# A two-layer hybrid decoder trunk on one core: forget logits two slots later, the first products of a normed operand in another order, six output chunks by halves

## The chip, the cores and the metric

The kernel runs on one core of one Trainium2 chip. The metric is the device time of one execution in microseconds (us). Each core has engines with instruction queues of their own: TensorE (PE in the profile, its weight loads are PEld), VectorE (DVE), ScalarE (ACT), GpSimd (POOL) and SyncE (SP), which here issues most of the DMAs.

## The reference

The input x has 512 positions of 1024 features in float32; there are two layers with their own weights.

```python
for l in range(DEPTH):
    mod = (c_act @ ada_w[l] + ada_b[l])[:, None, :]
    sh1, sc1, g1, sh2, sc2, g2 = jnp.split(mod, 6, axis=-1)
    h = rmsnorm(x, norm_mix_g[l]) * (1.0 + sc1) + sh1
    u = h @ w_in[l]
    fq, fk, fv, ff, pu, rq, rk, rv, rg, cu = jnp.split(u, bounds, axis=-1)
    y_fox = fox_attention(fq, fk, fv, ff, fox_fb[l])      # 4 heads of 64; log_sigmoid(ff) is summed over the positions
    y_pool = pool_mixer(pu, pool_w[l], pool_scale[l])
    y_ret = retention(rq, rk, rv, rg, positions, ret_gn_g[l])
    y_conv = conformer_conv(cu, conv_w[l], conv_b[l], conv_ln_g[l], conv_ln_b[l])   # depthwise, 31 taps
    mix = jnp.concatenate([y_fox, y_pool, y_ret, y_conv], axis=-1)
    x = x + g1 * (mix @ w_out[l])
    h = rmsnorm(x, norm_ffn_g[l]) * (1.0 + sc2) + sh2
    f = (jax.nn.silu(h @ ffn_w1[l]) * (h @ ffn_w3[l])) @ ffn_w2[l]
    x = x + g2 * f
return rmsnorm(x, final_g)
```

(The reshapes into heads are left out here.)

## The kernel before, in words

**Layout.** x is held transposed in `xT`, as eight chunks of 128 features by 512 positions. Each large product is made from three fp32r matmuls: every operand is split into a high part, rounded to fp32r, and a low part, the remainder. `mm3` issues high times high, high times low and low times high. For the normed operand the parts are `yh[k]` and `yl[k]`, k = 0 to 7; for a weight `wh` and `wl`; for an activation `ah` and `al`.

**Weights.** `plan` lists all weight tiles in order of use. `load_w` fetches one by DMA into `raw` (two buffers), casts it on ScalarE into `wh` (L179) and subtracts on VectorE into `wl` (L184); `wh` and `wl` have four buffers each. `take` hands out the next tile, `rel` gives a buffer back, which starts the load of a later tile.

**Order.** All of TensorE's instructions after the opening stand in program order (`keep_in_program_order`). On the other engines the framework's scheduler sets the order at build time. Work that is not a large product is written as generators: `fox_gen` (forgetting attention), `ret_gen` (retention), `conv_gen` (convolution), `ada_pe_gen` (the modulation vector of layer 0 on TensorE), and others. `slot()` stands between groups of products and lets each running generator advance by a rate: `r_...` in layer 0, `q_...` in layer 1. A rate of 1.3 means 1.3 steps a slot on average. A step runs from one `yield` to the next. `finish_bg` runs a generator to its end at once. `do_o`, the first half of the output projection, begins with `finish_bg([cg])`, which ends the convolution.

**Norm.** `Norm.chunk` squares and adds each finished chunk of `xT`, by halves of 256 positions. When the eighth chunk of a half is there, `pending` gets `sums` (token sums on TensorE, reciprocal root on VectorE and GpSimd) and then `finish` (the root is spread by TensorE; per chunk k: `mod_t` makes t on VectorE, `mod_hi` makes yh on ScalarE, `mod_lo` makes yl on VectorE). `flush(n)` takes n from each pending counter and runs what reaches zero; its calls stand between matmuls.

**Output projection, second half.** Of its eight chunks the first N1 are made together over all 512 columns, a few singly, and the last NH by halves of the columns, first all lower halves and then all upper halves, so that the lower half's norm can start while the upper halves are made. NH is 5 before.

**First products after a norm.** `group` makes four products (i = 0 to 3) that read the whole normed operand, lower half first, then upper half. It stands after norm 1 of layer 1 and after norm 2 of both layers. It is also used, by halves, for the last four chunks of the second feed-forward product.

**Forget logits.** `fox_gen` first runs `log_forget` on the logits ff (a chain of small VectorE and ScalarE instructions, L818 to L828), yields twice, and then sums the result over positions with twenty small matmuls (`sm<-cs,ff` and `sm<-ones,ff` in the trace).

Of the kernel before, what the change touches and what calls it, by code (L numbers as in the profile page):

```python
# [31 lines left out]
SEGS = (8, 7, 7)  # L32
PIECE = 1040
TW = 528
KN = {'GA': 3, 'GA1': 3, 'TR': 'V', 'NH': 5, 'NH1': 5, 'ST': ((0, 1), (1, 1), (2, 2), (4, 1), (5, 1), (6, 1), (7, 1)), 'MO': 'rk rq rv pu rg o o o o', 'MO1': 'rk rq rv pu rg o o o o', 'GK': 4, 'RD': 'sync', 'MM': 3, 'SM': 4, 'FB': 1, 'FB1': 1, 'OUTP': 0.0, 'FRONT': 1, 'FRONT1': 0, 'r_rot': 2, 'r_ada': 0.9, 'r_conv': 1.3, 'r_fox': 1, 'r_ret': 1, 'r_pool': 1, 'r_adaV': 0.4, 'q_conv': 1.3, 'q_fox': 1, 'q_ret': 1, 'q_pool': 1, 'q_adaV': 1, 'bP': 4, 'bPT': 2, 'bt': 3, 'brx': 2, 'bmx': 6, 'br8': 4, 'bpl': 3, 'brP': 4, 'bada': 3, 'bacs': 2, 'NR': 2, 'NW': 4, 'N1': 3, 'N11': 1, 'YLG': 9, 'SC': ('AVPPPGPA', 'GGPAVVPP', 'VVVVVVPP', 'VVVVVGVP', 'AAVPAVVP', 'VVVVVVVP', 'VVVVVVVP', 'AAVPAVVP'), 'SH': ('AVAPPPPP', 'VPPPPPAP', 'AAGAAAPP', 'AAAAAAPP', 'AAAAAAGP', 'AVVGAAVG', 'AAAAAAPP', 'AAAAAAPP'), 'MS': '', 'OF': {'lc': -1.907, 'lwq': -2.817, 'lw': -2.364, 'lh': -2.036, 'sc': -1.65, 'ds': 0.034, 'sh': -2.846, 'pc': -0.763, 'mc': -2.466, 'ph': -0.991, 'mh': 0.907, 't': 0.871, 'yh': -1.858, 'yl': 0.927, 'wh': -0.208, 'wl': -2.386, 'whq': -1.469, 'wlq': -0.219, 'mm': 0.333, 'mq': -0.566, 'dq': 0.84}, 'KB': (-4.084, -0.552, 1.672, 3.163, 4.202, 4.915, 6.134, 7.492), 'OA': (1, 0, 2, 3), 'OA1': (0, 1, 3, 2), 'OB': (1, 2, 0, 3), 'OB1': (1, 3, 0, 2), 'OUTP1': 3.0}
# [11 lines left out]
def trunk(ctx, tc, x, c, positions, ada_w, ada_b, norm_mix_g, norm_ffn_g, w_in, fox_fb,  # L47
# [240 lines left out]
    FULL = ((0, S),)  # L288
    HALF = ((0, H2), (H2, S))

    def group(n, th, tl, nk, cols, done):
        ws = [take() for _ in range(n)]
        banks = banks4()[:n]
        for (a, b) in cols:
            for i in range(n):
                h, lo = ws[i]
                for k in range(nk):
                    if k % 2:
                        flush()
                    mm3(banks[i][:, a:b], h[:, k], lo[:, k], th[k][:, a:b], tl[k][:, a:b],  # L300
                        k == 0, k == nk - 1)
                done(i, banks[i], a, b)
                if b == S:
                    rel()
                slot(2.0 * (b - a) / S)
# [74 lines left out]
    def ada_pe_gen(l, parts):  # L380

        js = [part * KD + jj for part in parts for jj in range(KD)]
        ld = [ada_load(l, js[0], 0, KD, 1), ada_load(l, js[1], 0, KD, 1)]
        acc = None
        for n in range(len(js) + 1):
            yield
            if acc is not None:
                pt = aux_cols(1)
                PE.matmul(pt, acc[:, 0:P], sel[:, 0:1], start=True, stop=True)
                ada_set(l, js[n - 1], 1, pt)  # L390
                gate1[0] += n == KD and l == 0
            if n == len(js):
                break
            r = ld.pop(0)
            pt = small()
            for half in range(2):
                for q in range(4):
                    k = 4 * half + q
                    PE.matmul(pt[32 * q:32 * q + 32, 0:P], cact[:, k:k + 1].to_broadcast([P, 32]), r[:, k],
                              start=half == 0, stop=half == 1)  # L400
            acc = tmp("pw")
            A.copy(acc, pt[:, 0:P])
            if n + 2 < len(js):
                ld.append(ada_load(l, js[n + 2], 0, KD, 1))
# [59 lines left out]
    def mod_t(l, i, k, u, v, rs):  # L464
        y = tmp("t", v - u)
        V.scalar_tensor_tensor(out=y, in0=xT[:, k, u:v], scalar=gs[l][i][:, k:k + 1], in1=rs,  # L466
                               op0=ALU.mult, op1=ALU.mult)
        return y
# [8 lines left out]
    def mod_lo(l, i, k, u, v, y):  # L477
        sh = shift(l, i, k)
        V.scalar_tensor_tensor(out=yl[k][:, u:v], in0=y, scalar=sh, in1=f(yh[k][:, u:v]), op0=ALU.add, op1=ALU.subtract)  # L479

    def modulate(l, i, k, u, v, rs):
        y = mod_t(l, i, k, u, v, rs)
        mod_hi(l, i, k, u, v, y)
        mod_lo(l, i, k, u, v, y)
# [635 lines left out]
    for l in range(DEPTH):  # L1120
# [166 lines left out]
        for si, nseg in enumerate(SEGS):  # L1287
# [102 lines left out]
```

## Time and profile before

| what | value |
|---|---|
| median of 3 runs | 1255.21 us (1253.73 to 1256.19) |
| the profiled execution: its own time | 1255.84 us |
| the profiled execution: its span | 1254.0 us |
| TensorE busy | 1204.4 us, 96% |
| VectorE busy | 735.8 us, 59% |
| ScalarE busy | 413.4 us, 33% |
| GpSimd busy | 71.8 us, 6% |
| mean granted clock of TensorE | 0.977 |

The span is the time from the first to the last instruction in the profile; the execution's own time is a little longer. Busy shares are means over stages with different limits. In a row of the timeline stand the start, the duration, the engine, the line, the operation, what it writes and reads, the shape and how many; in brackets, how long the engine sat idle before it and what ended that. The line of a TensorE row is that of the helper (L59), so such rows are told apart by the tiles that they name.

### The profile page before, as it was taken

What the parts mean: (1) busy time and instruction counts of PE and PEld (TensorE: products, weight loads), DVE (VectorE), ACT (ScalarE), POOL (GpSimd) and SP (SyncE); (2) the same over time, 40 slices, a digit from 0 to 9 for tenths busy, and PEclk for the clock granted to TensorE, in tenths of its full rate; (3) what the DMA queues carried; (4) which work ended last, traced back from release to release, by engine and by line L of the source; (5) the groups of instructions that cost most, each with busy time, mean ns of one, the idle gap of its engine ahead of it and who ended that gap; (6) DMA issues with size and microseconds to landing.
All of it is one profiled execution on the core that took longest, in us unless ns stands there. A gap on an engine that the chain in (4) does not pass through costs nothing.

```text
span 1254.0 us, 17311 instructions
## 1 busy us (share of the span) xinstructions
PE 1204.4 (96%) x6757; PEld 1000.4 (80%) x6757; DVE 735.8 (59%) x1314; ACT 413.4 (33%) x690; POOL 71.8 (6%) x146
## 2 busy tenths in 40 slices
PE   8997999989999999999989799998999999999997
PEld 8875776789888888888889777688988888888877
DVE  5869865577986373553467976747743333333333
ACT  5433344344222232132334334524432123213222
POOL 5401011001000000000000000100100000000000
PEclk7998999989999999999999989998999999999999
DMA  9785741226977363443333341222633323233321
GB/s 309 191 214 156 205 136 55 68 85 202 288 245 222 95 205 105 134 149 95 90 85 81 88 114 56 68 67 84 189 114 101 100 85 99 88 99 101 95 74 67
DMA packets 240873, 160.07 MB, mean 128 GB/s; under 512 B 7094, under 2 KB 221328, under 8 KB 240792
## 3 DMA queue, kind: packets, MB, share of 16 engines
q1 hardware_dynamic: 240616, 158.89, 43.1%
q8 instruction: 53, 0.87, 0.3%
q14 instruction: 28, 0.23, 0.1%
q10 hardware_dynamic: 176, 0.08, 0.0%
HBM read 154.74 MB, written 2.11 MB: 125 GB/s over the span
## 4 chain that ended last, share of the span: by engine, by line
PE 84%; DVE 8%; DMA 4%; ACT 2%; issue 1%; SPq 1%; POOL 0%; DVEq 0%; ACTq 0%; POOLq 0%
PE mm L59 74%; PE sm L59 8%; DVE hc L788 3%; DMA ad<-in_ada_w 1%; DMA raw<-in_w_in 1%; DVE wl L184 1%; PE aux L59 1%; PE sm L64 1%; ACT wh L179 1%; DMA rx<-rx 1%; DMA xn<-in_x 0%; DVE t L466 0%; DVE xT L1109 0%; DVE yl L479 0%; SPq L363 0%
## 5 line engine op out<-in xcount | busy, mean ns | idle before, releaser
L179 ACT CAST wh<-raw 128x1024 fp32r<-128x1024 f32 (+3 forms) x196 | 198.8, 1014 | 597.6 <-PE mm L59 423.5
L59 PE MATMUL mm<-yh,wh 128*128 128x512 f32 (+1 forms) x984 | 378.7, 388 | 7.9 <-ACT yh L475 7.9
L59 PE MATMUL mm<-yl,wh 128*128 128x512 f32 (+1 forms) x984 | 374.8, 381 | 4.3 <-DVE yl L479 4.3
L59 PE MATMUL mm<-yh,wl 128*128 128x512 f32 (+1 forms) x984 | 372.9, 379 | 0.0
L184 DVE TENSOR_TENSOR wl<-raw,wh 128x1024 fp32r<-128x1024 f32 (+3 forms) x196 | 231.8, 1183 | 159.2 <-ACT wh L179 148.8
L59 PEld LDWEIGHTS mm<-yh,wh 128*128 128x128 f32 x984 | 188.0, 192 | 46.6 <-ACT yh L475 8.7
L59 PEld LDWEIGHTS mm<-yl,wh 128*128 128x128 f32 x984 | 189.3, 192 | 39.7 <-DVE yl L479 5.5
L59 PEld LDWEIGHTS mm<-yh,wl 128*128 128x128 f32 x984 | 188.8, 192 | 36.4
L59 PE MATMUL mm<-ah,wh 128*128 128x512 f32 (+1 forms) x516 | 189.6, 368 | 0.0
L59 PE MATMUL mm<-al,wh 128*128 128x512 f32 (+1 forms) x516 | 188.3, 365 | 0.8 <-DVE al L521 0.8
L59 PE MATMUL mm<-ah,wl 128*128 128x512 f32 (+1 forms) x516 | 188.1, 365 | 0.0
L1109 DVE SCALAR_TENSOR_TENSOR xT<-mm,mod,xT 128x512 f32<-128x512 f32 (+1 forms) x86 | 58.0, 676 | 143.9 <-PE mm L59 143.8
L59 PEld LDWEIGHTS mm<-ah,wh 128*128 128x128 f32 x516 | 97.0, 188 | 17.7 <-issue 0.7
L59 PEld LDWEIGHTS mm<-al,wh 128*128 128x128 f32 x516 | 97.0, 188 | 17.7 <-DVE al L521 1.1
L59 PEld LDWEIGHTS mm<-ah,wl 128*128 128x128 f32 x516 | 97.0, 188 | 16.8
L1293 DVE TENSOR_TENSOR t<-t,mm 128x512 f32<-128x512 f32 x42 | 28.8, 687 | 109.1 <-PE mm L59 109.0
L788 DVE SCALAR_TENSOR_TENSOR hc<-hp,cwT,hc 128x512 f32<-128x512 f32 x120 | 83.2, 745 | 0.2
L339 DVE SCALAR_TENSOR_TENSOR acs<-ada,cact,acs 128x512 f32<-128x512 f32 x98 | 73.4, 749 | 6.0 <-DMA ada<-in_ada_w 3.4
L445 POOL TENSOR_TENSOR r<-r,mhalf 128x2 f32<-128x2 f32 (+3 forms) x16 | 20.1, 1255 | 625.2 <-DVE r L453 625.2
L475 ACT ACTIVATE yh<-t,mod 128x256 fp32r<-128x256 f32 (+1 forms) x56 | 27.8, 533 | 32.1 <-DVE t L466 29.8
L59 PE MATMUL mm<-wh,yh 128*128 128x256 f32 (+1 forms) x128 | 37.4, 292 | 0.0
L59 PE MATMUL mm<-wl,yh 128*128 128x256 f32 (+1 forms) x128 | 36.1, 282 | 0.0
(249 smaller groups left out, 1152.2 us busy)
## 6 DMA issues: line engine op xcount, KB each, us to landing
raw<-in_ffn_w SPq DMA_DIRECT2D x104, 512.0 KB, 3.9
ada<-in_ada_w SPq DMA_DIRECT2D x80, 512.0 KB, 4.6
raw<-in_w_in SPq DMA_DIRECT2D x32, 512.0 KB, 4.5
raw<-in_ffn_w SPq DMA_DIRECT2D x32, 448.0 KB, 3.7
ad<-in_ada_w SPq DMA_DIRECT2D x32, 256.0 KB, 5.8
raw<-in_w_out SPq DMA_DIRECT2D x32, 256.0 KB, 3.1
raw<-in_w_in SPq DMA_DIRECT2D x4, 520.0 KB, 7.1
xn<-in_x SPq DMA_DIRECT2D x4, 512.0 KB, 4.7
```

What stands on the lines that cost most here:

```text
L59: m = nc.tensor.matmul(*a, **kw)
L64: m = nc.tensor.transpose(*a, **kw)
L179: A.copy(h[:, 0:n], raw)
L184: V.tensor_tensor(out=lo[:, 0:n], in0=raw, in1=f(h[:, 0:n]), op=ALU.subtract)
L339: V.scalar_tensor_tensor(out=acc, in0=r, scalar=ck, in1=acc, op0=ALU.mult, op1=ALU.add)
L445: G.tensor_tensor(out=out_, in0=ms, in1=mhalf[:, 0:ms.shape[-1]], op=ALU.pow)
L475: A.activation(yh[k][:, u:v], y, AF.Identity, bias=shift(l, i, k), scale=1.0)
L788: V.scalar_tensor_tensor(out=hcs[j], in0=hps[j][:, t:t + S], scalar=cwT[:, l, j, t:t + 1], in1=hcs[j], op0=ALU.mult, op1=ALU.add)
L1109: V.scalar_tensor_tensor(out=xT[:, n, u:v], in0=b[:, u:v], scalar=mod[l][:, gcol + n:gcol + n + 1], in1=xT[:, n, u:v], op0=ALU.mult, op1=A ...
L1293: V.tensor_tensor(out=t_, in0=t_, in1=b3, op=ALU.mult)
```

## The change

It has these parts:

- `fox_gen` yields four times in place of twice between `log_forget` and the sums.
- `group` has a flag `first`, set at the three places after a norm. With it, the lower half goes k by k over all four products with the two terms that read yh, and then product by product over the terms that read yl. The upper half goes product by product, with all yh terms ahead of all yl terms.
- `finish` makes t and yh for all eight chunks and then yl for all eight; t lies in the `qk` buffers (four of 512 columns, two t each) in place of `t` (three buffers).
- The counters of `pending` and the arguments of `flush` go from 3, 4 and 1 to 18, 24 and 6 (4 inside the new loops).
- NH goes from 5 to 6, N1 of layer 0 from 3 to 2.
- `ada_pe_gen` collects eight columns in the `aux` bank and writes them to `mod` with one instruction.
- The rate of the convolution goes from 1.3 to 1.1 in layer 0 and from 1.3 to 1.2 in layer 1.

```diff
-KN = {... 'NH': 5, 'NH1': 5, ... 'r_conv': 1.3, ... 'q_conv': 1.3, ... 'N1': 3, ...}
+KN = {... 'NH': 6, 'NH1': 6, ... 'r_conv': 1.1, ... 'q_conv': 1.2, ... 'N1': 2, ...}
...
-    def group(n, th, tl, nk, cols, done):
+    def group(n, th, tl, nk, cols, done, first=False):
         ws = [take() for _ in range(n)]
         banks = banks4()[:n]
         for (a, b) in cols:
+            early_half = first and a == 0
+            if early_half:
+                for k in range(nk):
+                    for i in range(n):
+                        if i % 2 == 0:
+                            flush(4)
+                        h, lo = ws[i]
+                        PE.matmul(banks[i][:, a:b], h[:, k], th[k][:, a:b], start=k == 0, stop=False)
+                        PE.matmul(banks[i][:, a:b], lo[:, k], th[k][:, a:b], start=False, stop=False)
+                for i in range(n):
+                    h, lo = ws[i]
+                    for k in range(nk):
+                        if k % 4 == 0:
+                            flush(4)
+                        PE.matmul(banks[i][:, a:b], h[:, k], tl[k][:, a:b], start=False, stop=k == nk - 1)
             for i in range(n):
                 h, lo = ws[i]
-                for k in range(nk):
-                    if k % 2:
-                        flush()
-                    mm3(banks[i][:, a:b], h[:, k], lo[:, k], th[k][:, a:b], tl[k][:, a:b],
-                        k == 0, k == nk - 1)
+                if first and not early_half:
+                    for k in range(nk):
+                        PE.matmul(banks[i][:, a:b], h[:, k], th[k][:, a:b], start=k == 0, stop=False)
+                        PE.matmul(banks[i][:, a:b], lo[:, k], th[k][:, a:b], start=False, stop=False)
+                    for k in range(nk):
+                        PE.matmul(banks[i][:, a:b], h[:, k], tl[k][:, a:b], start=False, stop=k == nk - 1)
+                elif not first:
+                    for k in range(nk):
+                        if k % 2:
+                            flush(6)
+                        mm3(...)
...
             if acc is not None:
-                pt = aux_cols(1)
-                PE.matmul(pt, acc[:, 0:P], sel[:, 0:1], start=True, stop=True)
-                ada_set(l, js[n - 1], 1, pt)
+                m = (n - 1) % KD
+                if m == 0:
+                    at = aux_cols(KD)
+                PE.matmul(at[:, m:m + 1], acc[:, 0:P], sel[:, 0:1], start=True, stop=True)
+                if m == KD - 1:
+                    ada_set(l, js[n - KD], KD, at)
...
-                    pending.append([3, lambda u=u, v=v: self.sums(u, v)])
+                    pending.append([18, lambda u=u, v=v: self.sums(u, v)])
...
-            pending.append([4, lambda: self.finish(u, v, r)])
+            pending.append([24, lambda: self.finish(u, v, r)])
...
             rs = spread(r, 2)[:, 0:H2]
+            ys = []
             for k in range(KD):
-                modulate(self.l, self.i, k, u, v, rs)
+                if k % 2 == 0:
+                    t_ = tmp("qk")
+                y = t_[:, (k % 2) * H2:(k % 2) * H2 + H2]
+                mod_t(self.l, self.i, k, u, v, rs, y)
+                mod_hi(self.l, self.i, k, u, v, y)
+                ys.append(y)
+            for k in range(KD):
+                mod_lo(self.l, self.i, k, u, v, ys[k])
...
         lf = log_forget(l, v[:, :, 256:260])
-        yield
-        yield
+        for _ in range(4):
+            yield
```

More of the change, by code (lines that the diff above doesn't have):

```diff
@@ L34 @@
 TW = 528
-KN = {'GA': 3, 'GA1': 3, 'TR': 'V', 'NH': 5, 'NH1': 5, 'ST': ((0, 1), (1, 1), (2, 2), (4, 1), (5, 1), (6, 1), (7, 1)), 'MO': 'rk rq rv pu rg o o o o', 'MO1': 'rk rq rv pu rg o o o o', 'GK': 4, 'RD': 'sync', 'MM': 3, 'SM': 4, 'FB': 1, 'FB1': 1, 'OUTP': 0.0, 'FRONT': 1, 'FRONT1': 0, 'r_rot': 2, 'r_ada': 0.9, 'r_conv': 1.3, 'r_fox': 1, 'r_ret': 1, 'r_pool': 1, 'r_adaV': 0.4, 'q_conv': 1.3, 'q_fox': 1, 'q_ret': 1, 'q_pool': 1, 'q_adaV': 1, 'bP': 4, 'bPT': 2, 'bt': 3, 'brx': 2, 'bmx': 6, 'br8': 4, 'bpl': 3, 'brP': 4, 'bada': 3, 'bacs': 2, 'NR': 2, 'NW': 4, 'N1': 3, 'N11': 1, 'YLG': 9, 'SC': ('AVPPPGPA', 'GGPAVVPP', 'VVVVVVPP', 'VVVVVGVP', 'AAVPAVVP', 'VVVVVVVP', 'VVVVVVVP', 'AAVPAVVP'), 'SH': ('AVAPPPPP', 'VPPPPPAP', 'AAGAAAPP', 'AAAAAAPP', 'AAAAAAGP', 'AVVGAAVG', 'AAAAAAPP', 'AAAAAAPP'), 'MS': '', 'OF': {'lc': -1.907, 'lwq': -2.817, 'lw': -2.364, 'lh': -2.036, 'sc': -1.65, 'ds': 0.034, 'sh': -2.846, 'pc': -0.763, 'mc': -2.466, 'ph': -0.991, 'mh': 0.907, 't': 0.871, 'yh': -1.858, 'yl': 0.927, 'wh': -0.208, 'wl': -2.386, 'whq': -1.469, 'wlq': -0.219, 'mm': 0.333, 'mq': -0.566, 'dq': 0.84}, 'KB': (-4.084, -0.552, 1.672, 3.163, 4.202, 4.915, 6.134, 7.492), 'OA': (1, 0, 2, 3), 'OA1': (0, 1, 3, 2), 'OB': (1, 2, 0, 3), 'OB1': (1, 3, 0, 2), 'OUTP1': 3.0}
@@ new lines @@
+KN = {'GA': 3, 'GA1': 3, 'TR': 'V', 'NH': 6, 'NH1': 6, 'ST': ((0, 1), (1, 1), (2, 2), (4, 1), (5, 1), (6, 1), (7, 1)), 'MO': 'rk rq rv pu rg o o o o', 'MO1': 'rk rq rv pu rg o o o o', 'GK': 4, 'RD': 'sync', 'MM': 3, 'SM': 4, 'FB': 1, 'FB1': 1, 'OUTP': 0.0, 'FRONT': 1, 'FRONT1': 0, 'r_rot': 2, 'r_ada': 0.9, 'r_conv': 1.1, 'r_fox': 1, 'r_ret': 1, 'r_pool': 1, 'r_adaV': 0.4, 'q_conv': 1.2, 'q_fox': 1, 'q_ret': 1, 'q_pool': 1, 'q_adaV': 1, 'bP': 4, 'bPT': 2, 'bt': 3, 'brx': 2, 'bmx': 6, 'br8': 4, 'bpl': 3, 'brP': 4, 'bada': 3, 'bacs': 2, 'NR': 2, 'NW': 4, 'N1': 2, 'N11': 1, 'YLG': 9, 'SC': ('AVPPPGPA', 'GGPAVVPP', 'VVVVVVPP', 'VVVVVGVP', 'AAVPAVVP', 'VVVVVVVP', 'VVVVVVVP', 'AAVPAVVP'), 'SH': ('AVAPPPPP', 'VPPPPPAP', 'AAGAAAPP', 'AAAAAAPP', 'AAAAAAGP', 'AVVGAAVG', 'AAAAAAPP', 'AAAAAAPP'), 'MS': '', 'OF': {'lc': -1.907, 'lwq': -2.817, 'lw': -2.364, 'lh': -2.036, 'sc': -1.65, 'ds': 0.034, 'sh': -2.846, 'pc': -0.763, 'mc': -2.466, 'ph': -0.991, 'mh': 0.907, 't': 0.871, 'yh': -1.858, 'yl': 0.927, 'wh': -0.208, 'wl': -2.386, 'whq': -1.469, 'wlq': -0.219, 'mm': 0.333, 'mq': -0.566, 'dq': 0.84}, 'KB': (-4.084, -0.552, 1.672, 3.163, 4.202, 4.915, 6.134, 7.492), 'OA': (1, 0, 2, 3), 'OA1': (0, 1, 3, 2), 'OB': (1, 2, 0, 3), 'OB1': (1, 3, 0, 2), 'OUTP1': 3.0}
@@ L294, in group @@
         for (a, b) in cols:
+            early_half = first and a == 0
[13 more added lines that the diff above has]
+                        PE.matmul(banks[i][:, a:b], h[:, k], tl[k][:, a:b], start=False, stop=k == nk - 1)
             for i in range(n):
                 h, lo = ws[i]
-                for k in range(nk):
-                    if k % 2:
-                        flush()
-                    mm3(banks[i][:, a:b], h[:, k], lo[:, k], th[k][:, a:b], tl[k][:, a:b],
-                        k == 0, k == nk - 1)
+                if first and not early_half:
[8 more added lines that the diff above has]
+                            flush(6)
+                        mm3(banks[i][:, a:b], h[:, k], lo[:, k], th[k][:, a:b], tl[k][:, a:b],
+                            k == 0, k == nk - 1)
                 done(i, banks[i], a, b)
@@ L462, in spread, with mod_t @@
         return pb
-    def mod_t(l, i, k, u, v, rs):
-        y = tmp("t", v - u)
+    def mod_t(l, i, k, u, v, rs, y=None):
+        y = tmp("t", v - u) if y is None else y
         V.scalar_tensor_tensor(out=y, in0=xT[:, k, u:v], scalar=gs[l][i][:, k:k + 1], in1=rs,
@@ L479, in mod_lo @@
         V.scalar_tensor_tensor(out=yl[k][:, u:v], in0=y, scalar=sh, in1=f(yh[k][:, u:v]), op0=ALU.add, op1=ALU.subtract)
[L481 to L484, printed above, removed]
     class Norm:
@@ L1127, in trunk @@
             cub = []
-            group(4, yh, yl, KD, HALF, put(cub))
+            group(4, yh, yl, KD, HALF, put(cub), True)
         hps = [conv_glu(cub[2 * j], cub[2 * j + 1]) for j in range(2)]
@@ L1274, in trunk @@
                     if q % 2:
-                        flush()
+                        flush(6)
                     prod_out(b, *tile_of(i), i, q, (0, 1, 4, 5)[q], u, v, q == 0, q == 3)
@@ L1301, in trunk @@
                 cur["on"] = 0.0
-                group(4, yh, yl, KD, HALF, put(bb))
+                group(4, yh, yl, KD, HALF, put(bb), True)
                 cur["on"] = 1.0
```

## The prediction

> **What bounds the kernel now.** I read the page first (busy shares, granted clock, chain), then what TensorE waited for, then the timelines of the engines around each of its longer waits.
>
> ```profile
> PE 1204.4 (96%) x6757; PEld 1000.4 (80%) x6757; DVE 735.8 (59%) x1314; ACT 413.4 (33%) x690; POOL 71.8 (6%) x146
> PEclk7998999989999999999999989998999999999999
> PE 84%; DVE 8%; DMA 4%; ACT 2%; issue 1%; SPq 1%; POOL 0%; DVEq 0%; ACTq 0%; POOLq 0%
> ```
>
> TensorE (PE) is busy for 96% of the span and carries 84% of the chain that ended last. Its order is written by hand, so whatever one of its instructions waits for, everything behind waits too. The change removes no large matmul; it can only shorten waits, and the half-speed clock that follows them. TensorE's waits, longest first (total, times, longest):
>
> ```profile
> PE sm L59 <- DVE ff L828: 13.6, 2, 7.8
> PE mm L59 <- ACT yh L475: 7.9, 5, 2.8
> PE aux L59 <- DVE mod L332: 5.3, 5, 2.1
> PE mm L59 <- DVE yl L479: 4.3, 5, 1.0
> ```
>
> They are the three things that the diff touches: forget logits (ff), normed operands (yh, yl), modulation vector (mod). Together 31.1 us, 2.5% of the span. One matmul costs:
>
> ```profile
> 934.30 287.63 PE mm L59 x1248
> 667.06 8.38 PE mm L59 x72
> ```
>
> With 512 columns 287.63/1248 = 0.2305 us, with 256 columns 8.38/72 = 0.1164 us, so a half costs half.
>
> **Part 1: forget logits two slots later.** The first three rows are layer 0 (TensorE, VectorE twice), the next two layer 1 (TensorE; the chain), the last two windows (width, TensorE busy, clock, DMA).
>
> ```profile
> 110.24 0.59 PE L59 MATMUL sm<-cs,ff 128*4 128x128 f32 x2 [5.76 <-DVE ff L828]
> 102.97 1.40 DVE L788 SCALAR_TENSOR_TENSOR hc<-hp,cwT,hc 128x512 f32<-128x512 f32 x2
> 109.93 0.16 DVE L828 SCALAR_TENSOR_TENSOR ff<-ff,ff 128x16 f32<-128x16 f32 x1
> 120.74 0.28 PE L59 MATMUL aux<-sel,pw 128*128 128x1 f32 x2
> 722.44 0.59 PE L59 MATMUL sm<-cs,ff 128*4 128x128 f32 x2 [7.79 <-DVE ff L828]
> 726.87 9.03 PE mm L59 x36
> 110.24:114.21 3.97, 3.97 (x20) 0.56 0.02 4
> 722.44:726.80 4.36, 4.36 (x21) 0.50 0.00 0
> ```
>
> The tiny ff instructions stand between pairs of convolution taps (1.40 us a pair), VectorE being served in order of readiness; TensorE runs dry at 104.48 and 714.65 and then does the sums at clock 0.50 to 0.56, in 3.97 and 4.36 us (3.97 x 0.56 or 4.36 x 0.50, 2.2 at full clock). Two slots are 24 matmuls of 512 columns, 5.5 us, in layer 0 with an ada step in them.
> Layer 0: TensorE would arrive at about 110.6 (108.5 without the first wait of part 2, which lies ahead). ff is ready at 110.1 today; as TensorE now goes on, a weight split and a rotary multiply get in between, 1.8 us as an estimate (1.22 is the split's row below), so 111.9. With sums of 3.1 us (between 2.2 and 3.97) both slots and the sums are done at 115.0; today that point is at 120.74. Gain 5.7; bounds 3.7 (ff 2.9 us late, slow sums) and 8.4 (ff not late, fast sums).
> Layer 1: today 726.80 and 24 matmuls at 9.03/36, 732.8. Then: arrival at 720.2, ff at 722.4+2.0, sums 3.3, 727.7. Gain 5.1, bounds 3.1 and 8.2. A remnant of the wait stays in both. The later fox steps move along two slots each; they end two slots later in the output products, which have eight slots, so nothing is left over for the last products to wait on. The DMAs of cum move with them, at the same distance from their readers.
>
> **Part 2: one write of mod per eight columns.**
>
> ```profile
> 100.58 0.35 PE L59 MATMUL aux<-sel,pw 128*128 128x1 f32 x2 [2.14 <-DVE mod L332]
> 129.99 0.35 PE L59 MATMUL aux<-sel,pw 128*128 128x1 f32 x2 [1.16 <-DVE mod L332]
> 139.44 0.38 PE L59 MATMUL aux<-sel,pw 128*128 128x1 f32 x2 [0.85 <-DVE mod L332]
> ```
>
> The next aux matmul waits until VectorE has read the one before. With 3 reads in place of 24 that can happen twice. The wait at 100.58 lies ahead of the ff wait and is in part 1 already; 1.16 + 0.85 = 2.0 us come on top (bounds 0 and 2.0).
>
> **Part 3: six halves, then high terms first.** Halving one more chunk costs 24 x 0.1164 - 12 x 0.2305 = 0.03 us in each layer: nothing. The flush counts grow by six with their thresholds: sums and finish fall after the same numbers of matmuls. The finish stands 12 half matmuls (1.4 us) further ahead of the first products. Windows of the first products after norm 2 of layer 0 (A), norm 1 of layer 1 (B), norm 2 of layer 1 (C), then gaps and clock of A, the largest gap of B, the cast of the fourth weight at A, and VectorE's work, last the split of that weight at A, B and C:
>
> ```profile
> 270.85:301.25 30.40, 26.71 (x203) 26.00 (x202) 23.68 (x49) 12.94 (x22) 3.97 (x8) 0.89 0.45 141
> 646.94:678.32 31.38, 27.47 (x203) 26.86 (x202) 18.21 (x37) 12.00 (x21) 0.97 (x3) 0.89 0.29 80
> 867.61:898.28 30.67, 26.98 (x203) 26.27 (x202) 23.68 (x49) 12.95 (x22) 3.98 (x8) 0.89 0.47 147
> 272.13 0.38 PE L59 MATMUL mm<-yl,wh 128*128 128x256 f32 x1 [1.01 <-DVE yl L479]
> 275.39 0.58 PE L59 MATMUL mm<-yh,wh 128*128 128x256 f32 x1 [1.96 <-ACT yh L475]
> 276.69 0.58 PE L59 MATMUL mm<-yl,wh 128*128 128x256 f32 x1 [0.72 <-DVE yl L479]
> 276.00:277.00 1.00, 0.31 (x1) 0.50 0.99 291
> 650.98 0.38 PE L59 MATMUL mm<-yh,wh 128*128 128x256 f32 x1 [2.82 <-ACT yh L475]
> 270.93 1.04 ACT L179 CAST wh<-raw 128x1024 fp32r<-128x1024 f32 x1 [0.54 <-PE sm L59]
> 268.56 1.26 DVE L466 SCALAR_TENSOR_TENSOR t<-xT,gs,sm 128x256 f32<-128x256 f32 x3
> 271.60 1.27 DVE L479 SCALAR_TENSOR_TENSOR yl<-t,mod,yh 128x256 fp32r<-128x256 f32 x3
> 273.18 1.22 DVE L184 TENSOR_TENSOR wl<-raw,wh 128x1024 fp32r<-128x1024 f32 x1
> 650.55 1.23 DVE L184 TENSOR_TENSOR wl<-raw,wh 128x1024 fp32r<-128x1024 f32 x1 [0.67 <-ACT wh L179]
> 869.95 1.22 DVE L184 TENSOR_TENSOR wl<-raw,wh 128x1024 fp32r<-128x1024 f32 x1
> ```
>
> 192 matmuls at 0.1164 and about 1.1 for sums and spread make 23.4 us; the three windows last 92.5, so 22.3 are lost: 11.3 with TensorE idle (30.40 - 26.71 and so on), 11.0 at half clock, 3.7 a site. Three t at once, then a split, then three yl: the three buffers of t and the yl behind each starve the products. The change takes that away, since eight t need no buffer back and the first 64 products no yl.
> But what is late next is the fourth weight. Product 8 already needs its low part, 0.8 us after the last product of the tail (E = 270.85, 646.94, 867.61), where today it was needed after 72. Its buffer comes free only at E, and its split ended at E+3.5, E+4.8 and E+3.5. Left where it is, it costs gaps of 2.7, 4.0 and 2.7. In readiness order eight t and several yl now stand ahead of it; I take 1 us more, 12.4 in all. For the clock I take 2.7 a site, nearer to the 1.8 and 2.2 that the sums after the ff gaps lost. Then 20.5 in place of 22.3: gain 1.8, taken as 1.5. Best bound: cast and split straight after E, 2.3 us, gaps 1.5 at A and C without a clock loss, B 4.0 + 2.7: 9.7, gain 12.6. Worst: all of eight t, eight yl and the other waiting VectorE work ahead, 10.9 us from E-3.4, split done at E+7.4: gaps 6.6, clock as today, 30.9, loss 8.6. Buffers qk and their last readers are long done at all three places.
>
> **Part 4: rates of the convolution.** A convolution takes 37 steps. In layer 0 it sees 29 slots before the output products: 29 x 1.3 = 37 steps, today it just ends; 29 x 1.1 = 31. The steps with the mean, the squares, their sums, the spread and the split of mix 6 and 7 are then issued in one burst ahead of the first output product, with no products between. The rows of the same steps today:
>
> ```profile
> 198.66 0.69 DVE L801 TENSOR_TENSOR t<-t,t 128x512 f32<-128x512 f32 x1
> 209.86 1.05 PE L59 MATMUL aux<-ones,t 128*128 128x1 f32 x8
> 211.19 1.01 POOL L445 TENSOR_TENSOR r<-r,mhalf 128x4 f32<-128x4 f32 x1 [4.50 <-DVE r L453]
> 216.74 1.14 PE L59 MATMUL sm<-ident,r 128*128 128x128 f32 x8
> 224.70 1.28 DVE L521 TENSOR_TENSOR al<-hc,ah 128x512 fp32r<-128x512 f32 x2
> 225.43 0.50 PE L59 MATMUL mm<-al,wh 128*128 128x512 f32 x1 [0.78 <-DVE al L521]
> ```
>
> TensorE's own work only moves. Its new gaps: mean to sums two subtractions (1.28, as the pair in the row of 224.70), a square and the 0.69 sum, 2.8 us as an estimate; sums to spread 1.3 (POOL 1.01 and hops); spread to the split mix 6, today 7.5 us from 217.9 to 225.4 among other work and 4.1 if it ran alone, less 1.4 for six products that need only mix 2 and 3. That is 6 to 9 less today's 0.78, and the clock 1 to 3: bounds 5 and 12, taken as 7.5, nearer to the lone chain, since fewer other steps are left there. In layer 1 there are 32 slots x 1.2 = 38 steps; the spread moves from slot 28 to slot 31, with 6.3 us of cover left for a chain of 4 to 7.5: 0.5 lost (0 to 1.5).
>
> **The sum.** 5.7 + 5.1 + 2.0 + 1.5 - 7.5 - 0.5 = 6.3 us. The profiled execution took 1255.84 (span 1254.0), 0.6 above the median of 1255.21; 1255.84 - 6.3 = 1249.5, and the median scale gives 1248.9. I say 1249.
>
> **Rivals.** (1) The fourth split comes straight after E and the gaps stay short: part 3 gains 12.6, 1238.4. For it: the cast stood only 0.1 us behind E at A (270.93). Against it: VectorE serves by readiness. Chance 0.10.
> (2) A gap of 3 us in one piece does not lower the clock at A and C: 5.4 more, 1244. Against it: in A the longest gap is 1.96 and the clock still fell to 0.50. Chance 0.10. The Trainium skill (TensorE: Matmul & The Clock Gate, Part 1: The HAM clock gate) has half clock only after a whole idle window of about 3.4 us; by that rule A would have kept its clock today, which this trace contradicts, and the sum would come to this rival's time.
> (3) The burst costs 12: sum 1.8, 1254, no change. For it: 7.5 us were needed today from spread to split. Chance 0.20.
> (4) Slower: the fourth weight's split sinks to the end of VectorE's queue at each norm. Loss 8.6 in place of a gain of 1.5, 1259.6. The balance turns at about E+6.8. For it: the split of 273.18 stood behind the three yl of 271.60 although its cast was through at 271.97. Against it: with all yh early, TensorE needs only that one split. Chance 0.17.
>
> **How the numbers follow.** The forecast case (1244 to 1253) has 0.40, the rivals 0.57, the rest 0.03. A measurement can tell about 0.2%, 2.5 us. Faster: 0.40 + 0.10 + 0.10; no change 0.20; slower 0.20. The range 1240 to 1259 leaves out half of (1) and half of (4).
>
> **What would show it.** The ff waits fall from 5.76 and 7.79 to 2 to 5 each; mod waits nearly vanish; waits for yh and yl at the three norms give way to one wait each for wl; between 215 and 235 us TensorE shows new gaps of 2 to 4 us on t, r and ah. Wrong it would be if the burst's gaps are absent, if wl does not appear as a releaser, or if the ff waits go entirely, sums at full clock.

## The result and the profile after

The changed kernel takes 1268.92 us (median of 4 runs, 1268.17 to 1271.03) against 1255.7 for the kernel before on the same chip (1253.73 to 1257.96): a ratio of 1.0107, 95% interval 1.0085 to 1.0129. It is 13 us slower; 1249, faster, was forecast, and the range to 1259 does not hold it. The profiled run took 1268.17, its span is 1266.4.

From the page of the changed kernel: busy times, granted clock by slices, the chain.

```profile
PE 1211.8 (96%) x6781; PEld 1008.8 (80%) x6781; DVE 735.6 (58%) x1295; ACT 411.4 (32%) x690; POOL 76.7 (6%) x146
PEclk8999899898999999999999989999999999999999
PE 81%; DVE 9%; DMA 5%; ACT 2%; SPq 2%; issue 1%; POOL 1%; DVEq 0%; ACTq 0%; POOLq 0%
```

Of the 12.4 us by which the span grew (1254.0 to 1266.4), TensorE is busy for 7.4 (1204.4 to 1211.8) and idle for the other 5.0. The work is the same (one more chunk is split into halves, 24 matmuls more), so nearly all of the 7.4 are put down to matmuls at half clock (the mean granted clock fell from 0.977 to 0.972). TensorE's share of the chain fell from 84% to 81%: more of the end is set by others.

What TensorE waited for in the changed kernel (total, times, longest), the rows that this text uses, the counterpart of the four rows shown of before:

```profile
PE sm L59 <- DVE wl L184: 10.2, 3, 3.8
PE sm L59 <- DVE ff L857: 9.9, 2, 6.8
PE mm L59 <- DVE wl L184: 3.7, 3, 1.3
PE aux L59 <- DVE t L830: 3.2, 1, 3.2
PE sm L59 <- ACT P L907: 2.7, 1, 2.7
PE mm L59 <- ACT yh L501: 2.3, 2, 1.4
PE mm L59 <- ACT ah L549: 1.7, 1, 1.7
PE aux L59 <- DVE mod L355: 1.2, 2, 0.9
```

The old waits shrank as the diff meant them to: ff 13.6 to 9.9, mod 5.3 to 1.2, yh 7.9 to 2.3, yl 4.3 to none. In their place stand waits that were not there: the split of a weight (wl, 13.9 in all), the convolution's t and ah, and a P of the attention (2.7).

The same places in each trace, counted from the span's start, less the time of the kernel before (minus is earlier). Each is the start of a matmul; the end of a window is the start of the product behind it. E is, as in the prediction, the place where the tail of the output products is done. A lead on a place in the middle is partly work put off behind it; E at A counts all. The opening itself differs by up to 2 us from trace to trace, so differences under 2 say nothing.

| place | before | after | p_fox | p_foxret | p_rates | u_rates | a_ret | a_both |
|---|---|---|---|---|---|---|---|---|
| layer 0, first pu product | 168.02 | -2.6 | -2.6 | -5.3 | -0.5 | -2.5 | -7.9 | -7.5 |
| layer 0, last rg product | 220.25 | -6.0 | +0.1 | -2.9 | -4.3 | +0.9 | -6.8 | -6.3 |
| layer 0, first output product | 222.47 | +4.0 | -0.1 | -4.4 | +5.1 | +0.7 | +2.4 | -7.7 |
| E at A | 270.85 | +9.8 | +5.8 | -0.9 | +7.3 | +6.2 | +9.1 | -4.1 |
| end of window A | 301.08 | +11.9 | +5.9 | -0.4 | +7.6 | +7.8 | +12.1 | -1.3 |
| E at C | 867.61 | +10.6 | +1.4 | -4.2 | +6.2 | +8.0 | +8.6 | -3.2 |
| end of window C | 898.12 | +12.3 | +1.9 | -3.7 | +7.0 | +10.3 | +10.2 | -0.8 |

(The kernels beside "after" are the experiments below.) Nearly all of the loss, 11.9, is there by the end of A; layer 1 adds nothing to speak of.

### The profile page after: what moved, and what is told of

Read it like the earlier page. It is cut to its first block, busy times and chain, and to the rows that moved or that the text cites. A ratio compares the mean times of both kernels' runs of the same rounds, so it can differ in the third digit from the quotient of the medians.

```text
span 1266.4 us, 17346 instructions
## 1 busy us (share of the span) xinstructions
PE 1211.8 (96%) x6781; PEld 1008.8 (80%) x6781; DVE 735.6 (58%) x1295; ACT 411.4 (32%) x690; POOL 76.7 (6%) x146
## 4 chain that ended last, share of the span: by engine, by line
PE 81%; DVE 9%; DMA 5%; ACT 2%; SPq 2%; issue 1%; POOL 1%; DVEq 0%; ACTq 0%; POOLq 0%
PE mm L59 71%; PE sm L59 8%; DVE hc L817 2%; DVE wl L184 2%; DMA raw<-in_w_in 2%; DMA ad<-in_ada_w 1%; DMA rx<-rx 1%; PE aux L59 1%; PE sm L64 1%; ACT wh L179 1%; DVE yl L505 1%; DVE qk L492 1%; SPq L962 1%; DMA xn<-in_x 0%; DVE xT L1138 0%
## 5 line engine op out<-in xcount | busy, mean ns | idle before, releaser
L59 PE MATMUL mm<-yh,wh 128*128 128x512 f32 (+1 forms) x984 | 374.3, 387 | 2.3 <-ACT yh L501 2.3
L59 PE MATMUL mm<-yh,wl 128*128 128x512 f32 (+1 forms) x984 | 369.2, 379 | 3.7 <-DVE wl L184 3.7
L59 PE MATMUL mm<-yl,wh 128*128 128x512 f32 (+1 forms) x984 | 348.8, 376 | 0.0
L59 PEld LDWEIGHTS mm<-yl,wh 128*128 128x128 f32 x984 | 176.2, 189 | 34.2 <-issue 1.0
L59 PE MATMUL mm<-wh,yl 128*128 128x256 f32 (+1 forms) x128 | 36.8, 288 | 0.0
```

Of the source, the lines that this page charges most:

```text
L59: m = nc.tensor.matmul(*a, **kw)
```

## The experiments

They were timed in five groups, each against the kernel before on the same chip. The kernel before took 1256.31 in the first group (p_fox, p_rates, p_norm, p_ada), 1255.54 in the second (u_rates, p_foxret, a_pm, n_pm), 1256.57 in the third (a_ret, n_six, n_late, c_late), 1256.42 in the fourth (a_both, n_sums, c_ada, c_rates) and 1255.64 in the fifth (p_fox1, p_fox0). A difference between kernels of two groups can be off by the difference of these times, 1.0 at most.

**First: each part alone on the kernel before.** The edits are those of the diff: `p_fox` the four slots of `fox_gen`, `p_rates` the rates 1.1 and 1.2, `p_norm` six halves and the new order of the norm with its flush counts, `p_ada` eight columns of mod at once.

> Kernel before with the two further yields alone. My theory: in layer 0 the forget sums are reached about 8 us earlier than now, and then about 8 us are lost again where the transposes of retention pair 0 come in the same slot as a softmax (the small PSUM banks are not free): the wait for the exponential of 2 to 3 us and half clock after it appears near 130 to 150 us. Net within 3 us of before: 1253 to 1258. Rival (the stall in the changed kernel comes from the other parts, not from the shift): the gain stays, 1244 to 1248.

> Kernel before with the convolution's rates 1.1 and 1.2 alone. My theory: the end of the convolution comes in one burst ahead of the first output product of layer 0, TensorE waits 2 to 3 us each for the squares' sum, the root and the split of mix 6, at half clock: 7 to 9 us slower, 1262 to 1265. Rival (fewer taps early help the forget logits and pay for the burst): 1253 to 1258.

> Kernel before with the norm's parts alone (six halves, N1 of 2, t and yh ahead of yl, first products with the high terms first). My theory: the fourth weight's split is needed 0.8 us after the tail and comes 6 us after it; the first products after norm 2 lose about 2 us in each layer, those after norm 1 nothing: 3 to 5 us slower, 1258 to 1261. Rival (high terms first removes the waits for yh and yl, and the losses at these places in the changed kernel come from what lies ahead of them): 1245 to 1252.

> Kernel before with the modulation vector written eight columns at a time, alone. My theory: the waits for mod (5.3 us in five) shrink to about one; those ahead of the forget sums are swallowed there: 2 to 4 us faster, 1251 to 1253. Rival (all of it is swallowed by the waits behind): no change, 1255 to 1256.

| part alone | median us | ratio, 95% interval |
|---|---|---|
| p_fox | 1257.43 | 1.0013 (0.9996 to 1.0030) |
| p_rates | 1264.22 | 1.0064 (1.0049 to 1.0080) |
| p_norm | 1260.69 | 1.0036 (1.0022 to 1.0051) |
| p_ada | 1258.53 | 1.0021 (1.0009 to 1.0033) |

No part gains. Against 1256.31 they lose 1.1 (not told from nothing by its interval), 7.9, 4.4 and 2.2, 15.6 together where the whole loses 13.2. The first three times lie in the bands of their theories. The modulation missed both expectations: its waits were all but gone from the trace (0.3 left of 5.3), and yet it was slightly slower.

**Second: layer 0, where TensorE's lead goes.** In p_fox TensorE runs ahead after the sums and is back to a lead of 2.6 at the first pu product. Between lies the first pair of the retention. Its products q times k in the timelines of the kernel before, the changed kernel and p_fox, in this order:

```profile
150.14 1.16 PE L59 MATMUL sm<-qk,qk 64*128 64x128 f32 x16
144.21 2.08 PE L59 MATMUL sm<-qk,qk 64*128 64x128 f32 x16 [2.70 <-ACT P L907]
144.27 2.08 PE L59 MATMUL sm<-qk,qk 64*128 64x128 f32 x16 [2.33 <-DVE qk L938]
```

Before, TensorE came to them at 150.14, waited for nothing and did them in 1.16. In the changed kernel it is there 8 us sooner (144.21 less the wait of 2.70 is 141.5), in part because attention products now stand behind these instead of ahead of them. It waits, and does the sixteen in 2.08, at half clock (0.50). VectorE is late for both waits: in p_fox the wait ended on the rotated q (qk), not on the exponential that was expected; in the changed kernel it ended on the attention's P, which had itself waited 0.65 for an mx of VectorE. VectorE's share of the stretch in the kernel before (columns: width, then busy time of PE, PEld, DVE, ACT, POOL, each with its count; clock, DMA share, GB/s):

```profile
90.00:168.00 78.00, 68.08 (x628) 53.98 (x627) 71.11 (x173) 31.06 (x71) 8.91 (x17) 0.96 0.64 175
```

71.11 of 78.00 is 91%, more than TensorE's 87%: here VectorE is nearly the bound, and a TensorE that no longer waits at one place waits for VectorE at the next. Four kernels tested it.

```diff
-        for _ in range(3 - 2 * pair):     # ret_gen
+        for _ in range(5 - 2 * pair):     # p_foxret: on p_fox; a_ret: on the changed kernel
```
```diff
-'r_conv': 1.1 ... 'q_conv': 1.2
+'r_conv': 1.3 ... 'q_conv': 1.3     # u_rates: on the changed kernel; a_both: with ret_gen as above
```

> The kernel before with the forget logits' four slots, and with the start of both retention pairs two slots later as well (5 - 2*pair in place of 3 - 2*pair). Theory (the earlier TensorE stalls at the first retention pair, whose rotated q is ready only at about 144 us, and gives the gain back there): the stall of 6.5 between the first rv product and the first pu product is gone, 1249 to 1253. Rival (it meets the next late operand further on, in the later retention steps or in the output products): 1255 to 1258, with the waits moved.

> The changed kernel with the two rates of the convolution set back to 1.3; everything else as changed. Theory (the burst in layer 0 is a loss by itself, as the rates alone on the kernel before showed with +8): 1259 to 1262, TensorE's waits on t, r, ah and al in front of the first output product of layer 0 fall from about 9 in all to 2 or less. Rival (the burst only takes up idle time that the earlier fox sums brought forward, so the parts overlap): 1264 to 1267.

> The changed kernel with the start of the retention pairs two slots later (5 - 2*pair). Theory (the stall at the first retention pair costs the whole change the same as it cost the fox part alone, where this edit brought 4.6): 1262 to 1266 against 1268.9 for the change. Rival (the burst and the output products of layer 0 take the time anyway, the parts not being additive): 1267 to 1271.

> The changed kernel with both edits at once: the convolution's rates back to 1.3 and the retention pairs two slots later. Each alone brought 1.5 to 2.8. Theory (TensorE comes early in layer 0 and then meets, one behind the other, the first retention pair and the burst of the convolution; whichever is left takes the time that the other no longer takes, so only both together give it back): 1256 to 1261. Rival (a third loss in layer 0 that neither edit touches): 1263 to 1266.

- p_foxret 1252.83, ratio 0.9971 (0.9959 to 0.9983): 4.6 better than p_fox and faster than before, as the theory said. The products q times k start at 151.85 there, with no wait and at full clock:

```profile
151.85 1.16 PE L59 MATMUL sm<-qk,qk 64*128 64x128 f32 x16
```

- u_rates 1266.12, ratio 1.0070 (1.0051 to 1.0090): only 2.8 back, in the rival's band.
- a_ret 1267.42, ratio 1.0084 (1.0059 to 1.0108): 1.5 back; my theory missed, the rival held.
- a_both 1255.40, ratio 0.9991 (0.9981 to 1.0002): 13.5 back, more than the 4.3 of the two single edits together. This is the hand-over that was expected, with 0.6 more gained than its band allowed.

The table shows it. With the retention moved alone, the lead grows to 7.9 at pu and still stands at 6.8 at the last rg product; then the convolution's burst takes 9.2 (to +2.4 at the first output product). With the rates back alone there is no burst, but the retention has already taken the lead. The burst's rows in the changed kernel, then in a_ret:

```profile
221.88 1.52 PE L59 MATMUL aux<-ones,t 128*128 128x1 f32 x8 [3.18 <-DVE t L830]
224.73 2.07 PE L59 MATMUL sm<-ident,r 128*128 128x128 f32 x8 [1.34 <-POOL r L471]
231.04 0.50 PE L59 MATMUL mm<-ah,wh 128*128 128x512 f32 x1 [1.73 <-ACT ah L549]
```

```profile
219.99 1.77 PE L59 MATMUL aux<-ones,t 128*128 128x1 f32 x8 [3.76 <-DVE t L830]
223.10 2.07 PE L59 MATMUL sm<-ident,r 128*128 128x128 f32 x8 [1.34 <-POOL r L471]
229.41 0.50 PE L59 MATMUL mm<-ah,wh 128*128 128x512 f32 x1 [1.98 <-ACT ah L549]
```

The three gaps are those that the prediction named, on t, r and ah; they are a chain of the convolution's own steps and last as long however early TensorE comes. The price of the rates then depends on what lies ahead: the steps taken out before the last rg product gave 4.3 back in p_rates, but only 0.5 between a_both (-6.3) and a_ret (-6.8). So the rates cost 7.9 alone and 12.0 (1267.42 less 1255.40) where the retention does not wait.

The table shows one thing more. In p_fox the lead is gone at the last rg product, but the loss of 5.8 at E arises behind the first output product. The stretch from there to E at A in the kernel before, p_fox and p_foxret (columns as above), and the longest wait of TensorE in p_fox's:

```profile
222.46:270.85 48.39, 47.58 (x279) 40.72 (x277) 30.30 (x49) 16.70 (x31) 1.76 (x1) 1.00 0.25 77
222.37:276.62 54.25, 51.27 (x298) 43.09 (x297) 32.45 (x53) 19.76 (x37) 1.76 (x1) 0.97 0.23 68
218.10:269.91 51.81, 50.62 (x315) 42.85 (x314) 31.41 (x51) 18.55 (x35) 1.76 (x1) 1.00 0.24 72
225.82 0.50 PE L59 MATMUL mm<-ah,wh 128*128 128x512 f32 x1 [1.79 <-ACT ah L520]
```

Of the 5.9 more in p_fox, TensorE is idle for 2.2 (54.25 - 51.27 against 48.39 - 47.58). The other 3.7 are small products of the shifted generators, which now stand behind the first output product, and a lower clock. p_foxret has as much of the put-off work (3.0 more busy time, at full clock) and only 0.4 more idle time. The wait of 1.79 is that of an output product for a high part that ScalarE makes from the convolution's result; the longest wait in this stretch was 0.78 before. u_rates loses 5.5 in the same stretch, with the same wait (1.8).

**Third: which layer the forget logits gain in.** p_foxret was split by layer (`4 if l else 2` and `5 if l else 3` in p_fox1, the reverse in p_fox0).

> The kernel before with the four fox slots and the retention two slots later in layer 1 alone; layer 0 as before. Theory (in layer 0 VectorE is busy for 91% of the 78 us around the forget logits, so that TensorE's wait there is VectorE's backlog and its removal is worth 1 at most; the gain of both layers together, 2.7 to 3.7, is layer 1's): 1251.5 to 1254.5. Rival (half of the gain is layer 0's): 1254.5 to 1257.

> The same edit in layer 0 alone. Theory (VectorE's backlog): 1254.5 to 1257, no change that can be told. Rival (the 5.7 that the prediction gave to layer 0 comes once the retention is out of the way): 1250 to 1253.

p_fox1 1253.55, ratio 0.9981 (0.9968 to 0.9994): layer 1, with the retention moved too, is worth 2.1, as the theory said. p_fox0 1254.39, ratio 0.9989 (0.9977 to 1.0002): 1.2 gained, just under the theory's band, not told from nothing by its interval, and far from 5.7.

**Fourth: the norm.** In the changed kernel, the windows A, B and C of the first products:

```profile
280.68:313.13 32.45, 27.36 (x203) 26.76 (x202) 21.93 (x45) 11.28 (x21) 3.01 (x7) 0.84 0.38 116
658.82:690.03 31.21, 26.16 (x203) 25.56 (x202) 17.97 (x36) 11.75 (x21) 0.80 (x3) 0.89 0.31 84
878.20:910.58 32.38, 27.30 (x203) 26.70 (x202) 22.21 (x46) 11.26 (x21) 3.31 (x7) 0.89 0.38 120
```

96.04 in all against 92.45. TensorE's gaps at A, the longest gaps at B and C, and VectorE's queue at A:

```profile
282.73 0.38 PE L59 MATMUL mm<-yh,wl 128*128 128x256 f32 x1 [1.30 <-DVE wl L184]
287.03 0.58 PE L59 MATMUL sm<-yh,wl 128*128 128x256 f32 x1 [3.79 <-DVE wl L184]
665.38 0.58 PE L59 MATMUL sm<-yh,wl 128*128 128x256 f32 x1 [2.58 <-DVE wl L184]
884.53 0.58 PE L59 MATMUL sm<-yh,wl 128*128 128x256 f32 x1 [3.79 <-DVE wl L184]
277.60 3.21 DVE L492 SCALAR_TENSOR_TENSOR qk<-xT,gs,sm 128x256 f32<-128x256 f32 x8
281.46 1.22 DVE L184 TENSOR_TENSOR wl<-raw,wh 128x1024 fp32r<-128x1024 f32 x1
282.99 1.27 DVE L505 SCALAR_TENSOR_TENSOR yl<-qk,mod,yh 128x256 fp32r<-128x256 f32 x3
284.57 1.26 DVE L505 SCALAR_TENSOR_TENSOR yl<-qk,mod,yh 128x256 fp32r<-128x256 f32 x3
285.76 1.22 DVE L184 TENSOR_TENSOR wl<-raw,wh 128x1024 fp32r<-128x1024 f32 x1
287.68 1.48 DVE L522 TENSOR_TENSOR P<-P,PT 128x256 f32<-128x256 f32 x3
```

The split of the third weight (281.46) ends at 282.68, E + 2.0, and the first gap waits for it. The split of the fourth (285.76) ends at 286.98, E + 6.3, behind eight t, the third split and six yl. Behind it still stand the last yl and the sums of squares (P) of the upper half. Five kernels took this apart.

```diff
# a_pm (on the changed kernel), n_pm (on p_norm): high-part terms weight by weight
-                for k in range(nk):
-                    for i in range(n):
-                        if i % 2 == 0:
+                for i in range(n):
+                    for k in range(nk):
+                        if k % 2 == 0:
                             flush(4)
# n_sums (on p_norm), n_late (on n_pm): the upper half's token sums later
-pending.append([18, lambda u=u, v=v: self.sums(u, v)])
+pending.append([18 if u == 0 else 60, lambda u=u, v=v: self.sums(u, v)])
# n_six: the kernel before with 'NH': 6, 'NH1': 6, 'N1': 2 alone
```

> The changed kernel with the high-part terms of the lower half issued weight by weight (eight products of one chunk, then those of the next), so that the fourth weight is needed 48 products, 5.6 us, later. Theory (the gap at A and C is the fourth weight's split, which stands behind eight t and part of the yl): the gaps before yh,wl of 3.8 at A and C fall under 1, 1260 to 1265. Rival (VectorE serves the split later still, or the yl of the same half become the late operand): 1267 to 1270, with the gap moved to yl or to the fourth chunk.

> The normed operand's part alone on the kernel before (six halves, high terms first, the t of all eight chunks ahead of the yl), with the high-part terms issued weight by weight. Theory: without the wait on the fourth weight the part gains what the high terms first were to bring; 1250 to 1256 against 1260.7 for the same part in the order of the change. Rival: the gap moves to yl or to the fourth chunk, 1258 to 1262.

> The kernel before with six output chunks by halves and nothing else of the norm part (no high terms first, t and yl chunk by chunk as before). Theory (the halves are free, as the prediction had it, and the loss of the norm part is the order of VectorE's work at the norm): 1254 to 1257. Rival (the sixth chunk by halves is itself what costs): 1258 to 1261.

> The norm part alone on the kernel before in the order of the change (weight by weight inside each chunk of the operand, so that the fourth weight is needed at product 8), with the token sums of the upper half asked for 40 counts later. Theory (both early demands, the fourth weight and the sums, must go before the gap does): the wait for the fourth weight stays at 3 to 5, 1256 to 1261. Rival (the early sums alone were the fault): 1246 to 1251, as with both.

> The norm part alone on the kernel before, high terms weight by weight, and the token sums of the upper half asked for 40 counts later, that is after 56 products in place of 16. Theory (VectorE has about 6 us of work behind the tail, whichever of it TensorE asks for first is the gap; with the fourth weight and the sums both asked for late the gap has cover): the wait of 5.5 before the sums falls to 2 or less at each norm, 1253 to 1258 against 1262.3. Rival (the low terms' yl or the upper half's spread take the gap over): 1260 to 1264.

| kernel | median us | ratio, 95% interval |
|---|---|---|
| a_pm | 1270.44 | 1.0126 (1.0107 to 1.0146) |
| n_pm | 1262.29 | 1.0050 (1.0031 to 1.0069) |
| n_six | 1254.62 | 0.9984 (0.9966 to 1.0002) |
| n_sums | 1261.88 | 1.0042 (1.0028 to 1.0057) |
| n_late | 1246.76 | 0.9923 (0.9896 to 0.9950) |

n_six: the halves are free, as forecast. a_pm and n_pm missed my theory: the low part of the fourth weight was asked for at product 50 in place of 8, so 42 products later (48 in the expectation). The waits on wl went, as that theory said, but nothing was gained, since the next early demand, the token sums, met the same queue; the rivals' times were nearer, but the gap moved neither to yl nor to the fourth chunk. The gap at A in n_pm:

```profile
281.21 1.01 PE L59 MATMUL aux<-ones,P 128*128 128x1 f32 x4 [5.53 <-DVE P L519]
```

n_sums asks for the sums later, but keeps the demand for the fourth weight: in its list of waits the rows on wl stand as in the changed kernel (10.2 and 3.7). It ended 0.9 above its theory's band; the wait stayed as that theory said. Only n_late, which puts both behind, gains: 15.5 against n_pm and 9.8 against the kernel before, 6 more than its theory's band allowed. Its windows A, B and C, then VectorE's and TensorE's rows at A:

```profile
269.72:297.60 27.88, 26.54 (x203) 24.58 (x202) 18.80 (x41) 11.26 (x21) 2.68 (x5) 1.00 0.33 105
643.27:670.02 26.75, 26.33 (x203) 24.52 (x202) 18.03 (x37) 11.21 (x21) 0.80 (x3) 1.00 0.36 97
859.50:887.40 27.90, 26.49 (x203) 24.53 (x202) 19.73 (x42) 11.27 (x21) 2.68 (x5) 1.00 0.37 115
274.77 1.22 DVE L184 TENSOR_TENSOR wl<-raw,wh 128x1024 fp32r<-128x1024 f32 x1
276.70 1.48 DVE L519 TENSOR_TENSOR P<-P,PT 128x256 f32<-128x256 f32 x3
278.24 0.61 PE L59 MATMUL aux<-ones,P 128*128 128x1 f32 x4 [0.77 <-DVE P L519]
```

82.53 in place of 92.45, 9.9 gained, with the granted clock at 1.00 throughout. The split ends no sooner than in the changed kernel: 275.99, E + 6.3 again. VectorE's order is the same; what changed is where TensorE first asks for its results.

**Fifth: the parts that gain, together.** c_late is p_foxret with the norm of n_late. c_ada is c_late with the modulation of the change; c_rates is c_late with the rates of the change.

> The same norm part with the late sums, together with the forget logits' four slots and the retention two slots later; convolution rates and modulation as before. If both theories hold and the parts add, 1248 to 1253; if the norm part keeps its loss, 1257 to 1261.

> The fastest version so far (fox four slots, retention two slots later, high terms weight by weight, late sums) with the modulation written eight columns at once as in the change. Theory (this part loses by itself, as it lost 2.2 alone): 1243 to 1246 against 1241.9. Rival (its waits on mod, 8.3 us in that version, go, and nothing else is hurt there): 1236 to 1240.

> The fastest version so far with the convolution's rates of the change, 1.1 and 1.2. Theory (the burst costs the more the earlier TensorE comes to it, since VectorE's steps of the convolution set its end): 1250 to 1257. Rival (it costs only what undoing it brought back in the changed kernel, 2.8): 1243 to 1246.

c_late 1241.92, ratio 0.9879 (0.9855 to 0.9903): the parts add (2.7 and 9.8 alone, 14.7 together), and this version beats both kernels. Its time lies 6 below the better of the two bands, as n_late's did. c_rates 1253.84, ratio 0.9965 (0.9950 to 0.9980): the rates cost 11.9 here, as the theory said. c_ada 1241.18, ratio 0.9881 (0.9864 to 0.9899): 0.7 below c_late, no difference that can be told; both expectations missed. Rows on mod and ff from the waits of c_late, then of c_ada:

```profile
PE aux L59 <- DVE mod L355: 8.3, 7, 2.2
PE sm L59 <- DVE ff L854: 6.8, 1, 6.8
```

```profile
PE sm L59 <- DVE ff L857: 10.0, 2, 6.8
PE aux L59 <- DVE mod L355: 2.6, 3, 1.2
```

Of the 5.7 that went from the wait on mod, 3.2 came back as a wait on ff: in layer 0 both are the same VectorE. In p_ada, too, the waits came back: on ff (13.6 to 15.2), on pw (0.7 to 2.9) and on mx (1.2, new). TensorE's idle time there is that of before (49.3 against 49.6), and its busy time is 3.1 longer for the same matmuls, so the 2.2 that it lost alone look like clock (0.975 against 0.977); at which place is not shown.

## Why the prediction was wrong, point by point

**Part 1, layer 0 (+5.7 forecast, 1.2 to be had, about 6 lost as made).** The place itself was sized well: ff was ready at 110.9 (111.9 forecast), a wait of 3.16 stayed (2 to 5 forecast), and both slots and the sums were done at about 113.2 (115.0 forecast). That the sums ran at full clock was luck: behind the same wait they ran at half clock in a_ret (last section). What failed is the sentence that the later steps "move along two slots each" and "nothing is left over". I looked at the one wait that went, and at the end of the generator, but not at the next place where TensorE needs VectorE. The retention did not move along, its rotated q comes from a VectorE at 91%, and the lead was gone by the last rg product; then the output products did wait, and 5.8 were lost by E at A (p_fox). Moving the retention too removes that loss (p_foxret). The gain that remains is small: of the 5.8 of the wait on ff, 1.9 came back as waits on mod (4.2 to 6.1 between 90 and 275 us, p_foxret). That the rest is VectorE's backlog is argued from the 91% and from p_fox0; no run with less work on VectorE tests it.

**Part 1, layer 1 (+5.1 forecast, 2.1 measured with the retention moved too).** TensorE's rows at the sums in the changed kernel:

```profile
738.61 0.59 PE L59 MATMUL sm<-cs,ff 128*4 128x128 f32 x2 [6.76 <-DVE ff L857]
738.99 1.49 PE L59 MATMUL sm<-ones,ff 128*4 128x128 f32 x6
```

Counted from the end of window B, TensorE came 5.5 later than before (731.85 - 690.03 against 714.65 - 678.32), as forecast, but ff came 4.5 later (738.61 - 690.03 against 722.44 - 678.32), where I had taken 2.0. The wait fell by 1.0 only, and the sums stayed at half clock. The wait was expected at 2 to 5 and is 6.76: the mis-sized term is how far VectorE lets ff slip once it is needed later.

**Part 2 (+2.0 forecast).** Alone 2.2 slower, 0.7 faster on the fastest version. The waits on mod went as forecast; that they would be worth their length was wrong: alone they came back on ff, pw and mx, and on the fastest version 3.2 of 5.7 came back on ff.

**Part 3 (+1.5 forecast, 4.4 lost alone).** The mechanism was right in its main term: the fourth weight's split is late next, behind the eight t and several yl. Two sizes were off. The third weight's split has no term in the sum; needed at product 6, it ended at E + 0.1 at A before (270.96) and at E + 2.0 in the changed kernel, and there are two waits on wl at each norm in place of one, 3.7 in all for the third weight. The fourth was mis-sized. I let it end at about E + 4.5 at A and C and E + 5.8 at B; the products that waited for it started at E + 6.3, 6.6 and 6.3, near the place of rival 4. The E + 6.8 at which I had the balance turn can only hold for the whole sum; by its own terms part 3 turns into a loss at about E + 5.5 (three gaps that end there, less 0.8 each, and 8.1 at half clock make the 22.3 of before). Idle time by the windows: 32.45 - 27.36 and so on, 15.2 in place of 12.4. Half clock: 96.04 - 15.2 - 70.2 (three times 23.4) is 10.6 in place of 8.1. Together 25.8 lost, against 20.5 forecast and 22.3 before: 3.6 more than before in these windows, 2.1 of it at A and 1.7 at C, while B is 0.2 shorter. Rival 1's time was out of reach by the split, but its gain was not: n_late reaches 9.9 of its 12.6 in these windows with the split as late as ever.

**Part 4 (-7.5 and -0.5 forecast).** Right alone: p_rates is 7.3 late at E of A and nothing more in layer 1, and the gaps on t, r and ah are where they were put, though two of them (1.3 and 1.7) are shorter than the 2 to 4 named. In the company of an earlier TensorE it costs 12.

**The sum.** Against the parts measured alone, part 1 was forecast at +10.8 and brought -1.1, part 2 +2.0 and -2.2, part 3 +1.5 and -4.4, part 4 -8.0 and -7.9: of the 21.9 between the two sums, 11.9 are part 1, the step that failed most. Rivals 3 and 4 together would have given 1264, still short of the measured time, and no rival doubted part 1. The sum also added terms that were each worked out as if the others were not there. In layer 0 the fox shift, the modulation and the burst all draw on the same VectorE and the same chain; the sum of the parts measured alone (15.6) differs from the whole (13.2), and undoing two parts one by one brought 4.3 where both together brought 13.5.

## What to carry to other kernels

A wait on a busy engine can be that engine's backlog: before a wait is priced as a gain, find the next thing that the released engine needs from the same queue, and how busy that queue is in this stretch. Where several results come late from one queue, moving one demand back brings nothing (n_pm, n_sums); move all of them behind work that needs none, and the gain comes at once without any change to the late engine (n_late). And undo parts in pairs as well as singly, since a loss can hide behind another.

## What the runs showed of the hardware that was not expected

The clock does not follow the length of one gap. The ff sums of layer 0 stand behind a single wait of 3.16 both in the changed kernel and in a_ret, and in both TensorE had been busy without a break, at a clock of 1.00, for the 3.4 us ahead of the wait. The row with the wait and the window of the sums, first in the changed kernel, then in a_ret:

```profile
110.89 0.38 PE L59 MATMUL sm<-cs,ff 128*4 128x128 f32 x2 [3.16 <-DVE ff L857]
110.50:113.30 2.80, 2.42 (x22) 1.82 (x22) 2.42 (x6) 0.03 (x1) 0.00 (x0) 1.00 0.61 180
```

```profile
111.00 0.58 PE L59 MATMUL sm<-cs,ff 128*4 128x128 f32 x2 [3.16 <-DVE ff L857]
111.00:113.20 2.20, 2.20 (x11) 1.35 (x12) 1.87 (x3) 0.00 (x0) 0.00 (x0) 0.50 0.67 198
```

The same wait left the clock at 1.00 once and at 0.50 the other time. Shorter gaps can do the same: the stretch at B in the changed kernel, with its gaps of 1.39, 1.08 and 2.58, and what followed.

```profile
660.00:665.00 5.00, 0.89 (x3) 0.48 (x3) 5.00 (x10) 2.89 (x6) 0.00 (x0) 0.76 0.40 112
665.00:668.00 3.00, 2.62 (x13) 2.62 (x13) 1.09 (x3) 0.00 (x0) 0.00 (x0) 0.50 0.60 153
```

After 0.89 us of work in 5.00 the clock was 0.50. By the rule of the Trainium skill (TensorE: Matmul & The Clock Gate, Part 1: The HAM clock gate), half clock comes after at least one idle window of about 3.4 us. The sums of the changed kernel agree with it; those of a_ret and the stretch at B came to half clock without a gap of that length. Neither the length of the gap nor the work ahead of it decides between the two runs of sums, and what does is not shown here. So the clock behind a gap of about 3 us can be put into a sum only as a range, as the prediction did with its 2.2 to 3.97.
